# Segment 0 split in halves, and the constants of dt and S5 and the first S5 tables queued later

## The chip, the core and the metric

The kernel runs on one core of one Trainium2 chip. The metric is the device time of one execution in microseconds; the median of several runs counts. The core's engines work from queues of their own, each in order: TensorE (PE, with its weight loads PEld), VectorE (DVE), ScalarE (ACT), GpSimd (POOL) and SyncE (SP), which here issues the transfers.

## What is computed

One layer of a hybrid recurrent decoder: RMSNorm of x, one input projection, three branches (an SSD scan, an RG-LRU scan, an S5 complex scan), each gated, then the output projection with the residual and a final RMSNorm. There are 2048 prompt rows and 64 sample rows of width 1024.

```python
h = rmsnorm(x, p['norm_g'])
proj = h @ p['w_in']
z, xbc, dt_raw, lru_x, lru_gate, s5_u, s5_gate = jnp.split(proj, SPLITS, axis=-1)
...
dt = jax.nn.softplus(dt_raw + p['ssd_dt_bias'])
a = -jnp.exp(p['ssd_a_log'])
...
ys5, s5_hr, s5_hi = s5_mixer(s5_u, p['s5_lambda_re'], p['s5_lambda_im'], p['s5_log_dt'], ...)
...
out = jnp.concatenate([y_ssd, y_lru, y_s5], axis=-1) @ p['w_out']
return x + out, ...
```

`s5_mixer` takes constants from its parameters alone (exp, sin and cos of `lambda * delta`, their powers, `bbar`); nothing of x goes into them. The same holds for `a` and for the scaled weights of dt.

## The kernel before

**Segments and blocks.** The rows are cut into `SEGS`: segments 0 to 3 of 512 prompt rows and segment 4 of the 64 sample rows, taken in the order `ORD = [0, 4, 1, 2, 3]`. The input projection's weights come as blocks of 128 columns (`Block`, line 181). A block is loaded as f32 into one of two `w32` buffers, its largest value (lines 194, 197) goes through TensorE (`bcast_scales`, the matmul of line 168) to a scale, and ScalarE (line 205) and VectorE (line 206) write its high and low f16 parts into `whl`, of which six exist. `w_ahead` traces the next block. `in_proj` (line 235) multiplies one block with one segment: per slice k of 128 input channels three matmuls (lines 247 to 249), high with high, high with low, low with high, 24 in all, into one of three PSUM banks.

**A segment's input.** `x_load` (line 263) loads tiles of 128 rows. `x_split` (line 289) takes them in pairs: ScalarE squares and sums (line 305), `rsqrt_of` makes the scale, VectorE applies it (line 308). Then for each k all four tiles are transposed on TensorE into one PSUM bank (line 312), ScalarE writes `XH` (line 314) and VectorE the rest `XL` (line 315), which frees the bank.

**The order of tracing.** In the loop over `ORD` (line 1247) segment i + 1 is split ahead of the S5 inputs of segment i (`s5_u`, line 791) and of some gates (`zgates`, whose VectorE step is line 363). At s == 2, that is i = 3, the kernel traces `x_split(3)`, the last split, and then `dt_w` (line 419: decay constants and scaled weights of dt) and `s5_consts` (line 809: exponentials by `exp_acc`, two Sin calls at lines 845 and 846, powers by `cmul` with lines 154 to 159, and `renorm`). At s == 3 it traces `s5_tables(sa, 0)` (line 901), the tables of the first S5 core, ahead of segment 3's S5 inputs: products on GpSimd (lines 912 to 935), transposes and small matmuls on TensorE (lines 944 and 950), eight transfers `TR<-K` (line 962), and the table `W` on VectorE and ScalarE (lines 967 to 980, with lines 978 and 979 for its upper halves). After the loop come `dt_seg` (small matmuls), `dt_finish` (the softplus, up to line 463), gates, `dt_sums` (from line 476), gates, and the four S5 cores (`s5_core`, line 997, first matmul line 1008). Tables b + 1 are traced behind core b; their scratch tiles share two slots, so their first product (line 912) needs a scratch tile of the tables before to be released.

**What sets the order on an engine.** The source's order is a priority, not the order itself: a planner (`schedule_with_timeline_sim=True`) goes through a simulated run, gives each engine the first-traced instruction among those that are ready at that moment, and writes each engine's queue from that. So work that depends on little is issued long before its place in the source. `behind(*ins)` (line 272) adds an edge from each instruction traced in it to the given one on the same engine: it is issued after that one. Instructions on other engines get no edge.

Of the kernel before, what the change touches and what calls it, by code (L numbers as in the profile page):

```python
# [8 lines left out]
F32 = mybir.dt.float32  # L9
# [12 lines left out]
D = 1024  # L22
KD = 8
# [19 lines left out]
def hymba_step_kernel(  # L43
# [191 lines left out]
    def in_proj(w, s):  # L235
# [10 lines left out]
        for k in range(KD):  # L246
            P.matmul(ps[:, :n], lhsT=w[:, 0, k, :], rhs=XH[s][:, k, :], start=(k == 0), stop=False)  # L247
            P.matmul(ps[:, :n], lhsT=w[:, 0, k, :], rhs=XL[s][:, k, :], start=False, stop=False)  # L248
            P.matmul(ps[:, :n], lhsT=w[:, 1, k, :], rhs=XH[s][:, k, :], start=False, stop=(k == KD - 1))  # L249
# [39 lines left out]
    def x_split(s):  # L289
# [8 lines left out]
        for q in range(0, len(rows), 2):  # L298
            pair = rows[q:q + 2]
            m = len(pair)  # L300
            ss = tmp.tile([128, 2], F32, name="ss2", tag="ss2", bufs=4)
            rs = tmp.tile([128, 2], F32, name="rs2", tag="rs2", bufs=4)
            for i, xt in enumerate(pair):
                sq = st.tile([128, D], BF16, name="xsq", tag="yhl", bufs=3)
                A.activation(out=sq[:n], in_=xt[:n], func=AF.Square, scale=D ** -0.5, accum_out=ss[:n, i:i + 1])
            rsqrt_of(rs[:n, :m], ss[:n, :m], n, XSC, m)()
            for i, xt in enumerate(pair):
                V.tensor_scalar(xt[:n], xt[:n], rs[:n, i:i + 1], None, op0=ALU.mult)
        for k in range(KD):
            ps = bank(*((ptp, "tp") if k % 2 else (pss, "gy"[k // 2 % 2])), "ps_xt")  # L310
            for i, xt in enumerate(rows):
                P.transpose(ps[:, 128 * i:128 * i + n], xt[:n, k * 128:(k + 1) * 128], id32[:n, :n])
            g = gcol[:, k:k + 1]
            A.activation(out=XH[s][:, k, :sn], in_=ps[:, :sn], func=AF.Copy, scale=g)
            V.scalar_tensor_tensor(XL[s][:, k, :sn], ps[:, :sn], g, XH[s][:, k, :sn], op0=ALU.mult, op1=ALU.subtract)
# [931 lines left out]
    for i, s in enumerate(ORD):  # L1247
        if 0 < i < 4:
            if i > 1:
                x_load(ORD[i + 1], xp)  # L1250
            x_split(ORD[i + 1])
        if s == 2:
            dt_w(dp)
            s5_consts(sk)
        if s == 3:
            xa.close()
            sa = pool(s5, "s5a", "left")
            tabs = s5_tables(sa, 0)
# [6 lines left out]
        zgates(GA[i])  # L1265
    for s in ORD:
        dt_seg(s)
# [196 lines left out]
```

## Time and profile before

| | us |
|---|---|
| median of 3 runs | 1663.81 |
| the runs | 1662.63 to 1663.87 |
| profiled execution | 1667.2 |
| its span | 1665.5 |
| busy: PE, DVE, ACT, POOL | 1580.5, 1114.9, 858.8, 542.2 |

The profile is of one execution; times count from its start. Rows of an engine in order of time give start, duration, source line, output <- inputs, count, and in brackets how long the engine sat idle before and what released it. Rows for windows give the busy time of PE, PEld, DVE, ACT and POOL, the granted TensorE clock as a share of full speed (PEclk), the mean busy share of the DMA engines and GB/s. A matmul's duration has its pipeline in it; neighbouring ones overlap.

### The profile page before, as it was taken

Reading aid. Unit: us, or ns where it says so; the run is one execution under the profiler, and the core shown is the slowest. Engines: PE = TensorE matmul, PEld = TensorE weight load, DVE = VectorE, ACT = ScalarE, POOL = GpSimd, SP = SyncE. Lnnn points to the kernel's source line nnn. Section 1 sums busy time; section 2 is a strip of 40 time slices with the busy share of each in tenths; the row PEclk is TensorE's granted clock in tenths of the full one; section 3 lists DMA queues with packets and bytes.
Section 4 is the critical chain, followed back from the end, with each engine's and each line's share of the span. In section 5 each row is a group of like instructions: output and inputs, shape, how many; then the busy total and the mean of one; then the engine's idle time right before and its main releaser. Section 6 shows DMA issues by size and latency. Waiting matters only on the chain.

```text
span 1665.5 us, 26647 instructions
## 1 busy us (share of the span) xinstructions
PE 1580.5 (95%) x9474; PEld 814.7 (49%) x9474; DVE 1114.9 (67%) x2643; ACT 858.8 (52%) x1913; POOL 542.2 (33%) x822
## 2 busy tenths in 40 slices
PE   6899899988989998999999999999999999999998
PEld 3554444444434444455555555555554544444443
DVE  7843579899486676578978967676777774533332
ACT  7834424434597776656656745466756352322210
POOL 1213316784032021155647545444444400000000
PEclk9999899999989999999999999999999999999999
DMA  7512322322232534333435433243335452533100
GB/s 242 136 47 52 97 101 90 90 84 88 85 118 73 150 112 112 99 86 98 141 111 140 134 96 101 65 134 109 108 114 160 136 184 92 187 102 101 45 26 33
DMA packets 143942, 178.18 MB, mean 107 GB/s; under 512 B 66424, under 2 KB 92480, under 8 KB 143808
## 3 DMA queue, kind: packets, MB, share of 16 engines
q1 hardware_dynamic: 143808, 176.47, 35.4%
q8 instruction: 75, 1.23, 0.3%
q14 instruction: 59, 0.48, 0.1%
HBM read 126.57 MB, written 48.69 MB: 105 GB/s over the span
## 4 chain that ended last, share of the span: by engine, by line
PE 44%; DVE 8%; ACT 3%; issue 2%; DMA 2%; POOL 1%; SPq 0%; POOLq 0%; ACTq 0%; DVEq 0%
PE ps_o L1180 7%; PE ps_o L1178 7%; PE ps_o L1179 7%; PE ps_mm L248 6%; PE ps_mm L247 6%; PE ps_mm L249 6%; DVE x L355 3%; PE ps_y L568 1%; PE ps_s L573 1%; PE ps_y L571 1%; PE ps_s L618 1%; DVE e L531 1%; PE ps_tp L545 1%; DVE x L642 1%; PE ps_o L1212 1%
## 5 line engine op out<-in xcount | busy, mean ns | idle before, releaser
L247 PE MATMUL ps_mm<-xh,whl 128*128 128x512 f16 x1280 | 493.7, 386 | 13.7 <-DVE pz L363 8.9
L249 PE MATMUL ps_mm<-xh,whl 128*128 128x512 f16 x1280 | 492.5, 385 | 0.9 <-DVE whl L206 0.9
L248 PE MATMUL ps_mm<-xl,whl 128*128 128x512 f16 x1280 | 493.1, 385 | 0.0
L248 PEld LDWEIGHTS <-whl 128*128 128x128 f16 x1600 | 155.9, 99 | 164.7 <-issue 33.6
L249 PEld LDWEIGHTS <-whl 128*128 128x128 f16 x1600 | 156.3, 99 | 152.1 <-issue 16.5
L247 PEld LDWEIGHTS <-whl 128*128 128x128 f16 x1600 | 159.2, 101 | 145.8 <-issue 16.3
L355 DVE SCALAR_TENSOR_TENSOR x<-raw,hcols,x 128x512 f32<-128x512 f32 x192 | 173.7, 905 | 37.1 <-ACT x L353 35.0
L1179 PE MATMUL ps_o<-wo,yt 128*128 128x512 f16 x512 | 194.0, 379 | 0.0
L1178 PE MATMUL ps_o<-wo,yt 128*128 128x512 f16 x512 | 193.9, 379 | 0.0
L1180 PE MATMUL ps_o<-wo,yt 128*128 128x512 f16 x512 | 193.7, 379 | 0.0
L1193 ACT ACTIVATE yt<-y,rsc 128x256 f16<-128x256 f32 (+1 forms) x144 | 56.8, 477 | 103.1 <-PE ps_o L1180 83.1
L524 ACT ACTIVATE e<-bcq,acum 128x128 f32<-128x128 f32 (+1 forms) x272 | 85.7, 386 | 34.5 <-PE ps_y L568 31.6
L538 POOL TENSOR_TENSOR ce<-ce,x 128x512 f32<-128x512 f32 x60 | 82.5, 1381 | 44.5 <-DMA ce<-eT 35.6
L641 ACT ACTIVATE th<-x 128x512 f32<-128x512 f32 x64 | 40.2, 628 | 101.5 <-DVE x L355 101.3
L1202 DVE SCALAR_TENSOR_TENSOR res<-ps_o,rsu,res 128x512 f32<-128x512 f32 x32 | 24.0, 750 | 98.6 <-PE ps_o L1180 98.6
L1367 ACT ACTIVATE yo<-res 128x1024 f32<-128x1024 f32 x16 | 16.8, 1050 | 133.0 <-DVE res L1202 133.0
L363 DVE SCALAR_TENSOR_TENSOR pz<-th,ps_mm 128x512 f32<-128x512 f32 x64 | 43.6, 682 | 54.3 <-ACT th L362 53.8
L1179 PEld LDWEIGHTS <-yt 128*128 128x128 f16 x512 | 50.2, 98 | 60.1
L1178 PEld LDWEIGHTS <-yt 128*128 128x128 f16 x512 | 50.2, 98 | 60.1
L1180 PEld LDWEIGHTS <-yt 128*128 128x128 f16 x512 | 50.1, 98 | 60.2 <-issue 0.2
L362 ACT ACTIVATE th<-ps_mm,sc_out 128x512 f32<-128x512 f32 x64 | 43.7, 683 | 63.5 <-PE ps_mm L249 63.0
L531 DVE TENSOR_TENSOR e<-e,gm 128x512 f32<-128x512 f32 (+1 forms) x68 | 55.9, 821 | 27.7 <-POOL gm L530 22.0
(449 smaller groups left out, 3018.6 us busy)
## 6 DMA issues: line engine op xcount, KB each, us to landing
w<-in_w_blk_dram SPq DMA_DIRECT2D x40, 512.0 KB
bcq<-aT SPq DMA_DIRECT2D x64, 256.0 KB
y<-ysp SPq DMA_DIRECT2D x16, 1024.0 KB
ce<-eT SPq DMA_DIRECT2D x60, 256.0 KB
xt<-in_x_dram SPq DMA_DIRECT2D x16, 512.0 KB
ysp<-x SPq DMA_DIRECT2D x32, 256.0 KB
wo<-in_w_out_dram SPq DMA_DIRECT2D x16, 512.0 KB
res<-in_x_dram SPq DMA_DIRECT2D x16, 512.0 KB
```

The lines of the kernel that those rows point to most:

```text
L247: P.matmul(ps[:, :n], lhsT=w[:, 0, k, :], rhs=XH[s][:, k, :], start=(k == 0), stop=False)
L248: P.matmul(ps[:, :n], lhsT=w[:, 0, k, :], rhs=XL[s][:, k, :], start=False, stop=False)
L249: P.matmul(ps[:, :n], lhsT=w[:, 1, k, :], rhs=XH[s][:, k, :], start=False, stop=(k == KD - 1))
L355: V.scalar_tensor_tensor(o, tap[j], w[j], o, op0=ALU.mult, op1=ALU.add)
L362: A.activation(out=th, in_=ps, func=AF.Tanh, scale=un2)
L524: A.activation(out=e[:n, h, :n], in_=bcq[:n, h, :n], func=AF.Relu, scale=-1.0, bias=acum[:n, c, 4 * g + h:4 * g + h + 1])
L531: V.tensor_tensor(e[:n, :, :n], e[:n, :, :n], gm.unsqueeze(1).to_broadcast([n, 4, n]), op=ALU.mult)
L538: G.tensor_tensor(ce[:, :, :n], ce[:, :, :n], CT[:, q0:q0 + n].unsqueeze(1).to_broadcast([128, 4, n]), op=ALU.mult)
L1178: P.matmul(ps, lhsT=h, rhs=w[:, 0, c], start=(k == 0), stop=False)
L1179: P.matmul(ps, lhsT=h, rhs=w[:, 1, c], start=False, stop=False)
L1180: P.matmul(ps, lhsT=l, rhs=w[:, 0, c], start=False, stop=(k == nk - 1))
L1193: A.activation(out=hl[:, k, 0, :n], in_=r[:, k, :n], func=AF.Copy, scale=c)
```

## The change

Three edits. `x_split` takes segment 0 in two halves of two row tiles, each with its own transposes, `XH` and `XL`, and `in_proj` multiplies the first block with segment 0 in the same two halves of 256 columns; all other segments and blocks stay as they were. `x_split` returns its last ScalarE and VectorE instruction, and `dt_w` and `s5_consts` are traced `behind` those of segment 3. `s5_tables(sa, 0)` is traced after the loop instead of at the start of its last pass.

```diff
@@ -243,10 +243,12 @@
                     b.finish()
             b.left = b.left or (b.w is w and s == 3)
         ps = bank(pmm, "mm", "ps_mm")
-        for k in range(KD):
-            P.matmul(ps[:, :n], lhsT=w[:, 0, k, :], rhs=XH[s][:, k, :], start=(k == 0), stop=False)
-            P.matmul(ps[:, :n], lhsT=w[:, 0, k, :], rhs=XL[s][:, k, :], start=False, stop=False)
-            P.matmul(ps[:, :n], lhsT=w[:, 1, k, :], rhs=XH[s][:, k, :], start=False, stop=(k == KD - 1))
+        first = s == 0 and w is WB[W_ORDER[0]].w
+        for c in (slice(0, n // 2), slice(n // 2, n)) if first else (slice(0, n),):
+            for k in range(KD):
+                P.matmul(ps[:, c], lhsT=w[:, 0, k, :], rhs=XH[s][:, k, c], start=(k == 0), stop=False)
+                P.matmul(ps[:, c], lhsT=w[:, 0, k, :], rhs=XL[s][:, k, c], start=False, stop=False)
+                P.matmul(ps[:, c], lhsT=w[:, 1, k, :], rhs=XH[s][:, k, c], start=False, stop=(k == KD - 1))
         return ps[:, :n]
 
     def seg_tile(tag, name, s, pool, w=SG, bufs=None, wsmp=NS):
@@ -295,24 +297,29 @@
             XL[s] = xpool.tile([128, KD, SG], F16, name="xl", tag="xs")
         n = min(128, sn)
         rows = [XT[s0 + o] for o in range(0, sn, 128)]
-        for q in range(0, len(rows), 2):
-            pair = rows[q:q + 2]
-            m = len(pair)
-            ss = tmp.tile([128, 2], F32, name="ss2", tag="ss2", bufs=4)
-            rs = tmp.tile([128, 2], F32, name="rs2", tag="rs2", bufs=4)
-            for i, xt in enumerate(pair):
-                sq = st.tile([128, D], BF16, name="xsq", tag="yhl", bufs=3)
-                A.activation(out=sq[:n], in_=xt[:n], func=AF.Square, scale=D ** -0.5, accum_out=ss[:n, i:i + 1])
-            rsqrt_of(rs[:n, :m], ss[:n, :m], n, XSC, m)()
-            for i, xt in enumerate(pair):
-                V.tensor_scalar(xt[:n], xt[:n], rs[:n, i:i + 1], None, op0=ALU.mult)
-        for k in range(KD):
-            ps = bank(*((ptp, "tp") if k % 2 else (pss, "gy"[k // 2 % 2])), "ps_xt")
-            for i, xt in enumerate(rows):
-                P.transpose(ps[:, 128 * i:128 * i + n], xt[:n, k * 128:(k + 1) * 128], id32[:n, :n])
-            g = gcol[:, k:k + 1]
-            A.activation(out=XH[s][:, k, :sn], in_=ps[:, :sn], func=AF.Copy, scale=g)
-            V.scalar_tensor_tensor(XL[s][:, k, :sn], ps[:, :sn], g, XH[s][:, k, :sn], op0=ALU.mult, op1=ALU.subtract)
+        step = 2 if s == 0 else 4
+        for q0 in range(0, len(rows), step):
+            part = rows[q0:q0 + step]
+            for q in range(0, len(part), 2):
+                pair = part[q:q + 2]
+                m = len(pair)
+                ss = tmp.tile([128, 2], F32, name="ss2", tag="ss2", bufs=4)
+                rs = tmp.tile([128, 2], F32, name="rs2", tag="rs2", bufs=4)
+                for i, xt in enumerate(pair):
+                    sq = st.tile([128, D], BF16, name="xsq", tag="yhl", bufs=3)
+                    A.activation(out=sq[:n], in_=xt[:n], func=AF.Square, scale=D ** -0.5, accum_out=ss[:n, i:i + 1])
+                rsqrt_of(rs[:n, :m], ss[:n, :m], n, XSC, m)()
+                for i, xt in enumerate(pair):
+                    V.tensor_scalar(xt[:n], xt[:n], rs[:n, i:i + 1], None, op0=ALU.mult)
+            c = slice(128 * q0, 128 * q0 + n * len(part))
+            for k in range(KD):
+                ps = bank(*((ptp, "tp") if k % 2 else (pss, "gy"[k // 2 % 2])), "ps_xt")[:, 0:n * len(part)]
+                for i, xt in enumerate(part):
+                    P.transpose(ps[:, 128 * i:128 * i + n], xt[:n, k * 128:(k + 1) * 128], id32[:n, :n])
+                g = gcol[:, k:k + 1]
+                last = [A.activation(out=XH[s][:, k, c], in_=ps, func=AF.Copy, scale=g),
+                        V.scalar_tensor_tensor(XL[s][:, k, c], ps, g, XH[s][:, k, c], op0=ALU.mult, op1=ALU.subtract)]
+        return last
 
 
     tails = const.tile([128, 20, 27], F32, name="tails")
@@ -1248,14 +1255,14 @@
         if 0 < i < 4:
             if i > 1:
                 x_load(ORD[i + 1], xp)
-            x_split(ORD[i + 1])
+            xs_last = x_split(ORD[i + 1])
         if s == 2:
-            dt_w(dp)
-            s5_consts(sk)
+            with behind(*xs_last):
+                dt_w(dp)
+                s5_consts(sk)
         if s == 3:
             xa.close()
             sa = pool(s5, "s5a", "left")
-            tabs = s5_tables(sa, 0)
             S.dma_start(out=st_all, in_=conv_st)
             lru_const(dp)
         for b in range(4):
@@ -1263,6 +1270,7 @@
             if s == 3:
                 w_ahead()
         zgates(GA[i])
+    tabs = s5_tables(sa, 0)
     for s in ORD:
         dt_seg(s)
     dta = dt_finish(dp)
```

## Rows read from the trace of the kernel before

**Rows 1.** windows of 50 us: us, busy time (instructions) of each engine, PEclk, DMA share

```profile
100.00:150.00 50.00, 50.00 (x292) 25.78 (x289) 11.22 (x29) 14.48 (x21) 12.73 (x17) 1.00 0.18 50
150.00:200.00 50.00, 42.61 (x455) 23.95 (x454) 25.81 (x76) 27.55 (x65) 18.39 (x22) 0.88 0.35 86
350.00:400.00 50.00, 50.00 (x281) 25.96 (x279) 47.04 (x122) 22.84 (x73) 31.34 (x52) 1.00 0.32 96
```

**Rows 2.** TensorE in order of time: start us, us, line, what [idle before <-releaser]

```profile
10.39 1.09 PE L312 MATMUL ps_xt<-id,xt 128*128 128x128 f32 x4 [0.70 <-DVE sc_m L115]
18.63 0.58 PE L247 MATMUL ps_mm<-xh,whl 128*128 128x512 f16 x1 [0.31 <-ACT xh L314]
20.98 0.63 PE L248 MATMUL ps_mm<-xl,whl 128*128 128x512 f16 x1
24.29 0.38 PE L248 MATMUL ps_mm<-xl,whl 128*128 128x512 f16 x1
```

**Rows 3.** groups by line, 0 to 60 us: form, count, busy us, mean ns

```profile
L315 DVE SCALAR_TENSOR_TENSOR xl<-ps_xt,gcol,xh 128x512 f16<-128x512 f32 x16 | 11.5, 744 | 0.4 <-ACT xh L314 0.4
L315 DVE SCALAR_TENSOR_TENSOR xsm<-ps_xt,gcol,xsm 128x64 f16<-128x64 f32 x8 | 2.2, 278 | 2.3 <-ACT xsm L314 2.3
L206 DVE SCALAR_TENSOR_TENSOR whl<-w,sc_out,whl 128x1024 f16<-128x1024 f32 x5 | 6.4, 1277 | 0.8 <-ACT whl L205 0.8
```

**Rows 4.** TensorE in order of time, 50 to 80 us

```profile
54.95 0.19 PE L247 MATMUL ps_mm<-xsm,whl 128*128 128x64 f16 x1 [1.23 <-ACT u L796]
75.44 3.20 PE L312 MATMUL ps_xt<-id,xt 128*128 128x128 f32 x12 [3.22 <-DVE xl L315]
```

**Rows 5.** VectorE in order of time, 71 to 76 us

```profile
71.54 2.05 DVE L308 TENSOR_SCALAR xt<-xt,rs 128x1024 f32<-128x1024 f32 x2
73.51 1.13 DVE L158 TENSOR_TENSOR uw<-s_tt 128x16 f32<-128x16 f32 x1
74.65 1.40 DVE L315 SCALAR_TENSOR_TENSOR xl<-ps_xt,gcol,xh 128x512 f16<-128x512 f32 x2
```

**Rows 6.** windows around two stalls, columns as in rows 1

```profile
72.00:84.00 12.00, 8.66 (x33) 4.60 (x32) 11.97 (x33) 7.59 (x13) 5.78 (x5) 0.72 0.11 44
174.00:184.00 10.00, 9.57 (x35) 4.36 (x36) 4.87 (x12) 4.57 (x8) 5.58 (x4) 0.66 0.47 131
```

**Rows 7.** ScalarE in order of time, 162 to 175 us

```profile
162.39 1.14 ACT L205 ACTIVATE whl<-w,sc_out 128x1024 f16<-128x1024 f32 x1
173.23 1.06 ACT L197 ACTIVATE whl<-w 128x1024 bf16<-128x1024 f32 x1 [0.77 <-DMA w<-in_w_blk_dram]
```

**Rows 8.** TensorE in order of time, 168 to 175 us

```profile
174.43 0.59 PE L168 MATMUL ps_sc<-w_mx,ones 128*128 128x1 f32 x2 [5.64 <-DVE whl L206]
```

**Rows 9.** VectorE in order of time, 119 to 171 us

```profile
119.37 2.73 DVE L315 SCALAR_TENSOR_TENSOR xl<-ps_xt,gcol,xh 128x512 f16<-128x512 f32 x4 [3.39 <-ACT xh L314]
147.62 0.16 DVE L154 TENSOR_TENSOR tW<-W,wpw 128x4 f32<-128x4 f32 x1
161.65 5.18 DVE L979 SCALAR_TENSOR_TENSOR W<-W,wpw,tW 128x128 f32<-128x128 f32 x4 [1.82 <-ACT tW L978]
166.75 2.25 DVE L206 SCALAR_TENSOR_TENSOR whl<-w,sc_out,whl 128x1024 f16<-128x1024 f32 x1
170.16 0.86 DVE L979 SCALAR_TENSOR_TENSOR W<-W,wpw,tW 128x128 f32<-128x128 f32 x3
```

**Rows 10.** GpSimd in order of time, 161 to 182 us

```profile
161.17 1.17 POOL L912 TENSOR_TENSOR tC<-Ct,Ap 128x576 f32<-128x576 f32 x1 [7.79 <-DMA TR<-K]
180.56 1.26 POOL L935 TENSOR_TENSOR AB<-tD 128x512 f32<-128x512 f32 x1
```

**Rows 11.** VectorE and TensorE in order of time, 221 to 236 us

```profile
221.22 0.44 DVE L463 TENSOR_TENSOR dtz<-dt_all,hd 128x272 f32<-128x272 f32 x1
226.23 0.59 PE L476 MATMUL ps_dt<-dtz,tri 128*128 128x256 f32 x2
235.89 1.12 PE L1008 MATMUL ps_s<-u,sl 128*64 128x264 f32 x8
```

## The prediction

> **What bounds the kernel now.** I read the windows of equal length first, then TensorE in order of time around each gap they show, then the engine that each gap names. From 350 us TensorE is busy in 50.00 of 50 us [rows 1], and so it is in most later windows: there it sets the pace. The change works ahead of that, where time is lost. Between 150 and 200 us it is busy in 42.61 with a mean granted clock of 0.88, against 50.00 and 1.00 between 100 and 150 us [rows 1]. Three places hold the loss. **The start:** the first projection matmul begins at 18.63 us, although transposes of the first two row tiles begin at 10.39 [rows 2]; `x_split` waits for all four tiles before any slice of `XH` exists. **The gap at 72 us:** 3.22 us of waiting for `XL` on VectorE [rows 4]; behind it the mean clock of 12 us is 0.72 [rows 6]. Below full speed it is at the lower of its two levels (1.2 of 2.4 GHz, so 0.5), and 12 x (1 - 0.72) = 3.4 us of work are lost on top. **The gap at 169 us:** 5.64 us [rows 8], then a clock of 0.66 over 10 us [rows 6], another 3.4 us.
>
> **The profiled execution** took 1667.2 us around a span of 1665.5; the median of the runs is 1663.8, 3.4 less. I make the sum against 1667.2 and take the same difference off the median.
>
> **A, the first segment in halves.** The transposes of tiles 0 and 1 stay where they are. They end at about 11.5 [rows 2]; with a half-width copy on ScalarE behind what it has queued there (`whl` of the same block among it) I put the first matmul at about 13 us. 512 columns at 2.4 GHz are 0.21 us, so a group of 24 matmuls is 5.1 us; its first half, 2.6 us of work, now fits before 18.63. The matmuls from 20.98 stand with 0.63 us in their rows and those from 24.29 with 0.38 [rows 2]: seven of them ran at the lower level, and earlier work may lift the clock before they come, up to 7 x 0.21 = 1.5 us. Between 18.63 and 20.98 there is at most 1.2 us of waiting that may go as well. So the upper end is 5.3. Against it stands VectorE, nearly full at that time: L315 takes 744 ns for 512 columns and 278 for 64 [rows 3], which makes 0.48 us for 256; sixteen of them cost 7.7 us in place of 5.9. If VectorE ends the second half, that is -1.7. About as many microseconds of constants leave the same queue, so I take **+3.5**, the 2.6 and part of the clock.
>
> **B, the constants queued behind the last split.** `behind` holds only instructions of ScalarE and VectorE: some 211 small VectorE ones of `dt_w` and `s5_consts` with a few of ScalarE. The six loads on SP's queue, GpSimd's memsets, copies and products and one TensorE matmul aren't held; the loads stay as early as now and cost nothing new, and the rest waits for its data. At 72 us VectorE had the row scaling L308 and then L158, a 16-column product of the constants that took 1.13 us, before `XL` L315 could start at 74.65 [rows 5]; without L158 and L159 it starts 1.1 us earlier. That is the lower end; the whole gap with its clock is 3.2 + 3.4 = 6.6. GpSimd's products of the constants leave this place too, and I take **+5**. ScalarE loses the two Sin calls, with the table loads that they bring, from a stretch in which TensorE once waits 1.23 us for it [rows 4]: 0 to 1.2, taken **+1**. Where the constants go, behind the last `XL` of segment 3 (the four that begin at 119.37 [rows 9], earlier by what is gained), VectorE is busy 11.22 of 50 us [rows 1]; 211 instructions of about the 0.16 us of a 4-column product [rows 9] are 34 us of busy time, where 39 of 50 are free. Queued behind them are the gates' `pz` (L363), for which TensorE's banks wait; three banks of 5.1 us each cover them, and I take 0 with 1 us as the other end.
>
> **C, the first tables behind the seg-3 projections.** The gap at 169 us is a chain. ScalarE ends `whl` L205 at 163.5 [rows 7]; VectorE's L206 for the same block starts only at 166.75, because four L979 of the tables take 5.18 us in front of it (three later ones take 0.86, so 0.29 each), and itself takes 2.25 [rows 9]. It frees the buffer for the next load, which ScalarE waits for until 173.23 [rows 7], and TensorE's L168 comes at 174.43. L206 takes 1.28 us earlier on [rows 3]; started at 163.5 it would end 4.2 us earlier and leave 1.4 of the gap. So 4.2 without the clock, 9.0 with everything, 0 if other table work lands there. I take **+6**, the 4.2 and half of the clock.
>
> **E, what the tables will hit instead.** GpSimd's work for the second tables starts at 161.17, when the transfers `TR<-K` of the first have released their scratch tile, and its twelve large instructions last until 180.56 and beyond [rows 10]. Later first tables make it later. In the old place it ran against L979 and L206; each of the four L979 lost (5.18 - 4 x 0.29) / 4 = 1.0 us there [rows 9]. In the new place it meets the softplus of dt, which ends at 221.22 with TensorE's sums waiting until 226.23 [rows 11]; the last product of that chain is over at 221.9, so 4.3 us of room. Half of the twelve hitting it costs 6 - 4.3 = 1.7 us and, if the clock falls, 3.4 more: **-5**, between 0 and 12 - 4.3 + 3.4 = 11.1.
>
> **Sum:** 3.5 + 5 + 1 + 6 - 5 = 10.5 us, 1656.7 for the profiled execution, 1653.3 for the median.
>
> **The rivals.** *No collision:* the planner lets TensorE take the tables' transposes early (it fills gaps between groups, as now), GpSimd is done before the softplus, and E is 0: 10.5 + 5 = 15.5 off, 1648. For it: nothing after 121 us but order keeps the tables back.
> *Full collision:* all twelve hit the softplus, E is 11.1, 1659. For it: dt's matmuls follow the first tables directly in the source. The Trainium skill says in "SBUF — State Buffer", section "Who interferes with whom", that a two-input VectorE instruction and a GpSimd one share a port pair which one of them holds to its end while the other fully blocks; by that rule each of the twelve stops one instruction, and this rival is the result. The L979 rows agree, 1.0 us lost by each.
> *Slower:* the W tables' VectorE chain, which now runs from 147.62 to 171.02 [rows 9], 23.4 us, is queued behind the softplus. That would end near 221.7 - 9.5 + 6 = 218 and W at 241.6, where the first S5 core's matmuls come at 235.89 now [rows 11]: 5.7 us later than before and 3.4 for the clock, 1673. It decides from the point where the last L979 ends later than about 230. Against it: VectorE has free time behind 119 us, and the constants' 34 us of busy time end by about 160 even if nothing in them overlaps.
> *A gap of C's size elsewhere:* TensorE's queue is ordered anew from 12 us on, and 9.0 us come back at another block: 1662.
> *The halves do nothing:* VectorE is the pace, A is 0: 1657.
>
> **Chances.** Forecast 0.46, no collision 0.16, full collision 0.16, slower 0.09, gap elsewhere 0.07, halves idle 0.06. 0.2% of the time, 3.3 us, is about what a measurement of this kernel can tell from no change. Faster than 1660.5 are the forecast, the first, the last and most of the full collision: 0.72. The gap elsewhere and the rest of those give within 0.2%: 0.15. Slower: 0.13, with a little for gaps that add up. The range goes from all gains at their upper ends (5.3 + 1.2 + 6.6 + 9.0 = 22 off, 1642) to the gap elsewhere plus a loss in A, 1666; it leaves out the slower rival.
>
> **What would show it.** In the new profile the first projection matmul stands at 12 to 14 us with 256 columns; no gap of 3 us stands near 72; no Sin table load before the last split; L206 of the blocks loaded behind segment 3 takes 1.3 us and L168 waits under 2 us for it; L912 of the second tables comes at 170 or later, and the softplus rows grow from 0.44 to over 1 us beside it. The first S5 core starts near 225. I am wrong if the first matmul still waits until 18 us, if the gap at 169 us only moves, or if the core starts no earlier than 235.

## The result and the profile after

The changed kernel takes 1672.05 us, median of 5 runs, where the kernel before takes 1663.81: a ratio of 1.0058, 95% interval 1.0046 to 1.0071. Measured once more (the run *changed*) it was 1.0044 (1.0027 to 1.0061). It is slower by about half a per cent, clear of the noise; forecast were 1653.3, between 1642 and 1666. The profiled execution took 1672.05 us around a span of 1670.3 (before: 1667.2 around 1665.5). That of before lay 3.4 us above its median and that of after on it, so the two traces differ by 4.9 us, not by the 8.2 of the medians.

To see where the time went I add up, in windows of 10 us, what TensorE loses: its idle time and its busy time x (1 - PEclk), the work that a lower clock costs. From kernel to kernel these sums follow the spans within 4 us. One part is missing in them: PEclk stands at 1.00 in the first windows, though matmuls still have the long rows of the lower level there (0.63 us at 20.98 in before [rows 2], 0.42 at 15.39 in after, below). Half of TensorE's busy time up to the clock's first record (23.7 us in before, 19.1 in after) is an estimate of what the first column leaves out: 4.8 us and 3.9.

```
lost on TensorE, us   0-100  100-150  150-200  200-240  240-450  450-1640   sum
before                 23.5      0.0     11.8      0.6     24.2      42.2  102.3
after                  17.5      0.5     16.2     10.9     20.2      42.2  107.5
difference             -6.0     +0.5     +4.4    +10.3     -4.0       0.0   +5.2
forecast               -9.5      0.0     -6.0     +5.0      0.0       0.0  -10.5
```

The third and the fourth stretch hold two things each. From 150 to 180 us, where the gap at 169 was, before loses 7.3 and after 9.3. Behind that come dt's small matmuls (L452, after L459; 189 to 199 us before, 183 to 192 after): with the lower clock behind them they cost 5.1 in before (180 to 210 us) and 7.0 in after (180 to 200). So the gap at 169 was replaced by one that is 2.0 us larger, and the 10.9 from 200 on are new.

The windows of after, columns as in [rows 1], show the same: where [rows 1] had a whole 50 us from 100 on, 0.46 are missing, 150 to 200 got worse, and of the 40 us from 200 on TensorE works 31.31.

```profile
100.00:150.00 50.00, 49.54 (x246) 24.27 (x244) 38.09 (x177) 17.27 (x25) 16.02 (x26) 1.00 0.14 38
150.00:200.00 50.00, 40.65 (x425) 22.66 (x426) 36.30 (x139) 22.84 (x58) 12.79 (x16) 0.83 0.35 86
200.00:240.00 40.00, 31.31 (x186) 15.86 (x184) 30.69 (x68) 9.51 (x17) 8.25 (x7) 0.87 0.25 83
```

The windows around stalls: the one at 72 us is nearly gone against [rows 6] (11.28 busy of 12, clock 1.00), and a new one stands at 190 to 210.

```profile
72.00:84.00 12.00, 11.28 (x60) 5.86 (x59) 9.65 (x17) 10.37 (x16) 1.91 (x4) 1.00 0.15 44
...
190.00:210.00 20.00, 9.52 (x101) 5.50 (x101) 19.48 (x38) 5.27 (x20) 10.68 (x11) 0.67 0.11 29
```

TensorE of after in order of time (L249 is before's L247, L318 its L312). The first projection matmul, 256 columns, stands at 12.89 instead of 18.63 [rows 2], and from 19.16 on such a matmul takes 0.27 us instead of 0.42, the full speed that before has in its row at 24.29 [rows 2]; the wait of 3.22 us at 72 [rows 4] is 0.71. The wait of 5.64 us at 169 [rows 8] isn't there, but one of 5.17 stands at 157 to 162 and one of 8.69 at 201 to 210. Both are put down to L115, the first VectorE step of a weight block's scale: it reads a sum that TensorE has left in a bank, and TensorE's next use of that bank waits for it.

```profile
12.89 0.37 PE L249 MATMUL ps_mm<-xh,whl 128*128 128x256 f16 x1 [0.28 <-ACT xh L320]
...
15.39 0.42 PE L250 MATMUL ps_mm<-xl,whl 128*128 128x256 f16 x1
...
19.16 0.27 PE L250 MATMUL ps_mm<-xl,whl 128*128 128x256 f16 x1
...
76.69 1.31 PE L318 MATMUL ps_xt<-id,xt 128*128 128x128 f32 x8 [0.71 <-DVE xl L321]
...
162.39 0.56 PE L168 MATMUL ps_sc<-w_mx,ones 128*128 128x1 f32 x2 [5.17 <-DVE sc_m L115]
...
209.96 0.58 PE L249 MATMUL ps_mm<-xh,whl 128*128 128x512 f16 x1 [8.69 <-DVE sc_m L115]
```

**The first new gap.** ScalarE had one block's squares at 146.5 and the next one's at 151.7, and then waited 11.01 us for the scale of the first, which L115 begins at 162.09; the matmul L168 at 162.39 is that of the next block and waited for the same L115 to free the bank:

```profile
146.35 0.18 ACT L197 ACTIVATION_READ_ACCUMULATOR whl<-w 128x1 f32 x1
...
151.51 0.19 ACT L197 ACTIVATION_READ_ACCUMULATOR whl<-w 128x1 f32 x1
162.71 1.15 ACT L205 ACTIVATE whl<-w,sc_out 128x1024 f16<-128x1024 f32 x1 [11.01 <-DVE sc_out L107]
```

VectorE in the same time, and again from 191 us. Up to 162.6 it has the constants' chain of dependent 16- and 32-column steps (L154 to L159, L809 to L812), with L115 in the middle of its last round. Some of the steps take 0.16 us, others 0.9 to 1.3 in the rows shown. From 191 on the same shows in W's chain (L986, before's L979), where eight take 4.23 us, and in the softplus: L467, L468, L123 and L124 take 1.94, 1.53, 1.04 and 1.14 us, where they take 0.44, 0.49, 0.30 and 0.30 in the run *held* below. L470 behind them has its usual 0.44 ([rows 11] has the same for L463).

```profile
155.51 1.24 DVE L155 TENSOR_TENSOR s_tt<-uw 128x16 f32<-128x16 f32 x1
156.68 0.16 DVE L156 TENSOR_TENSOR s_tt<-uw 128x16 f32<-128x16 f32 x1
...
158.97 1.29 DVE L810 TENSOR_TENSOR rn_t<-rn_t 128x16 f32<-128x16 f32 x1
...
162.09 0.15 DVE L115 TENSOR_SCALAR sc_m<-ps_sc 128x1 int32<-128x1 int32 x1
...
191.03 4.23 DVE L986 SCALAR_TENSOR_TENSOR W<-W,wpw,tW 128x128 f32<-128x128 f32 x8 [0.17 <-ACT tW L985]
195.18 1.94 DVE L467 TENSOR_TENSOR dtz<-d 128x272 f32<-128x272 f32 x1
...
197.15 1.53 DVE L468 SCALAR_TENSOR_TENSOR dtz<-dtz,dtun,hd 128x272 f32<-128x272 f32 x1
...
200.07 1.04 DVE L123 TENSOR_SCALAR ex_r<-sp_az 128x272 f32<-128x272 f32 x1
...
201.16 1.14 DVE L124 TENSOR_SCALAR ex_k<-ex_r 128x272 f32<-128x272 f32 x1
...
209.75 0.16 DVE L115 TENSOR_SCALAR sc_m<-ps_sc 128x1 int32<-128x1 int32 x1
...
211.34 0.67 DVE L370 SCALAR_TENSOR_TENSOR pz<-th,ps_mm 128x512 f32<-128x512 f32 x1
...
226.90 0.44 DVE L470 TENSOR_TENSOR dtz<-dt_all,hd 128x272 f32<-128x272 f32 x1
```

GpSimd, beside them: the first tables' products lie from 135.04 to 160.2 with a pause from 145.7 to 155.4, the second tables' (161.17 to 181.8 in [rows 10]) from 192.65 to 215.0. The long rows of VectorE stand beside these and not in the pauses.

```profile
135.04 1.15 POOL L919 TENSOR_TENSOR tC<-Ct,Ap 128x576 f32<-128x576 f32 x1
...
155.45 1.27 POOL L939 TENSOR_TENSOR AB<-tD 128x512 f32<-128x512 f32 x1 [9.73 <-DVE CA L931]
...
158.97 1.26 POOL L942 TENSOR_TENSOR AB<-tD 128x512 f32<-128x512 f32 x1
...
192.65 1.29 POOL L919 TENSOR_TENSOR tC<-Ct,Ap 128x576 f32<-128x576 f32 x1 [8.86 <-DMA dm<-in_s_d_dram]
...
213.62 1.34 POOL L942 TENSOR_TENSOR AB<-tD 128x512 f32<-128x512 f32 x1
```

I count as stretched the VectorE instructions of up to 272 columns that take over 0.6 us, and add what each takes above 0.18. Before, the constants (40 to 100 us) have 2 of them, 1.6 us in all. After, between 120 and 164 us, it is 14 and 11.8 us.

### The profile page after: what moved, and what is told of

Read it like the earlier page. It is cut to its first block, busy times and chain, and to the rows that moved or that the text cites. A ratio compares the mean times of both kernels' runs of the same rounds, so it can differ in the third digit from the quotient of the medians.

```text
span 1670.3 us, 26716 instructions
## 1 busy us (share of the span) xinstructions
PE 1579.0 (95%) x9498; PEld 814.9 (49%) x9498; DVE 1132.6 (68%) x2651; ACT 863.3 (52%) x1925; POOL 539.6 (32%) x822
## 3 DMA queue, kind: packets, MB, share of 16 engines
q8 instruction: 75, 1.23, 0.3%
## 4 chain that ended last, share of the span: by engine, by line
PE 47%; DVE 8%; ACT 4%; DMA 3%; issue 2%; POOL 1%; SPq 0%; ACTq 0%; POOLq 0%; DVEq 0%
PE ps_o L1185 7%; PE ps_o L1186 7%; PE ps_o L1187 7%; PE ps_mm L249 6%; PE ps_mm L250 6%; PE ps_mm L251 6%; DVE x L362 3%; PE ps_y L575 2%; PE ps_s L580 1%; PE ps_y L578 1%; PE ps_s L625 1%; DMA y<-ysp 1%; PE ps_tp L552 1%; DMA ce<-eT 1%; DVE e L538 1%
## 5 line engine op out<-in xcount | busy, mean ns | idle before, releaser
L249 PE MATMUL ps_mm<-xh,whl 128*128 128x512 f16 (+1 forms) x1288 | 494.2, 384 | 28.3 <-DVE sc_m L115 15.9
L251 PE MATMUL ps_mm<-xh,whl 128*128 128x512 f16 (+1 forms) x1288 | 493.9, 383 | 0.2 <-DVE whl L206 0.2
L250 PE MATMUL ps_mm<-xl,whl 128*128 128x512 f16 (+1 forms) x1288 | 493.7, 383 | 0.0
L249 PEld LDWEIGHTS <-whl 128*128 128x128 f16 x1608 | 160.1, 101 | 148.1 <-issue 17.7
L205 ACT ACTIVATE whl<-w,sc_out 128x1024 f16<-128x1024 f32 x40 | 45.7, 1142 | 45.8 <-DVE sc_out L107 45.8
```

Of the source, the lines that this page charges most:

```text
L205: A.activation(out=w[:, 0], in_=self.r, func=AF.Copy, scale=su[:, 0:1])
L249: P.matmul(ps[:, c], lhsT=w[:, 0, k, :], rhs=XH[s][:, k, c], start=(k == 0), stop=False)
L250: P.matmul(ps[:, c], lhsT=w[:, 0, k, :], rhs=XL[s][:, k, c], start=False, stop=False)
L251: P.matmul(ps[:, c], lhsT=w[:, 1, k, :], rhs=XH[s][:, k, c], start=False, stop=(k == KD - 1))
```

## The experiments

The theory after the reading (theory one): the constants' late chain, traced ahead of the blocks' scales, stands in front of L115 (first gap), and it carries the second gap too, since it makes the tables late. The rival: the tables' later place does. Theory two, which the later texts speak of, was formed after the run chain: the place in the source decides nothing at the first gap; the chain is late because GpSimd's products stretch its steps. Theory three, on the halves, stands in the text of quiet_whole. One table for all runs: ratio to the kernel before with its interval, the loss on TensorE by stretch as above (one execution each), the start of segment 3's transposes and of the first S5 core, in us.

```
                ratio (95%)              0-100 100-150 150-200 200-240 240-450 450-1640   sum  seg.3  core
before          1                         23.5    0.0    11.8     0.6    24.2     42.2   102.3  111.7 235.9
halves          1.0010 (0.9995-1.0024)    23.9    0.0    13.5     0.6    23.6     43.4   105.1  110.4 234.7
consts          1.0021 (1.0008-1.0034)    16.0    0.6    21.5     1.1    24.2     39.3   102.7  103.4 237.8
tables          1.0012 (0.9996-1.0027)    23.1    0.0    10.5    10.3    19.4     40.5   103.8  111.2 241.0
halves_consts   1.0018 (1.0005-1.0030)    17.9    0.0    22.2     3.8    21.7     37.1   102.6  105.6 242.4
halves_tables   1.0025 (1.0009-1.0041)    23.9    0.0    10.4     8.3    21.7     44.0   108.4  110.1 238.6
consts_tables   1.0034 (1.0021-1.0046)    17.0    0.6    16.0     8.3    20.2     47.6   109.8  103.7 238.8
changed         1.0044 (1.0027-1.0061)    19.4    0.0    15.0    11.6    19.1     42.3   107.4  107.4 244.0
held            1.0043 (1.0022-1.0064)    18.7    0.0    16.8     0.0    27.8     41.7   105.0  105.4 233.0
chain           1.0052 (1.0037-1.0067)    17.9    0.0    16.2    11.1    19.8     44.2   109.1  105.2 241.6
quiet           0.9986 (0.9975-0.9998)    20.1    0.0    13.9     4.5    18.5     46.6   103.7  106.5 239.0
quiet_again     1.0001 (0.9987-1.0015)    18.0    0.0    16.0     3.2    19.7     43.3   100.1  104.4 238.0
quiet_whole     1.0004 (0.9991-1.0017)    17.3    0.0    17.1     3.4    22.2     43.0   103.0  103.5 232.3
quiet_held      1.0007 (0.9994-1.0020)    20.3    0.0     8.3     0.0    29.8     47.4   105.8  107.4 225.2
mid             0.9995 (0.9986-1.0004)    18.5    4.3    12.8     1.0    23.5     41.0   101.1  105.6 235.2
wl              0.9980 (0.9967-0.9992)    22.4    0.0     7.7     0.0    22.1     41.2    93.5  110.5 233.9
mid_wl          0.9992 (0.9978-1.0005)    18.6    3.9     5.9     0.0    21.6     45.3    95.4  106.3 232.5
halves_wl       0.9989 (0.9973-1.0004)    23.6    0.0     7.9     0.0    21.2     46.4    99.1  110.5 233.8
```

Executions of one kernel lie up to 7 us from their median, once 12 (the profiled one of quiet was its slowest, 1668.1 at a median of 1662.9), so a single sum of this table is good to a few us; single stretches differ by more than that where it matters. The stretch behind 450 us moves by as much from run to run as the parts do ahead of it. Ratios measured twice, of the changed kernel (1.0058, 1.0044) and of quiet (0.9986, 1.0001), came out 0.0014 and 0.0015 apart, so a difference of that size between two rows tells little.

**The parts alone and in pairs.** Out of the changed kernel one or two of these were undone: the halves,

```diff
-        first = s == 0 and w is WB[W_ORDER[0]].w
+        first = False
...
-        step = 2 if s == 0 else 4
+        step = 4
```

the constants, and the tables:

```diff
-            with behind(*xs_last):
-                dt_w(dp)
-                s5_consts(sk)
+            dt_w(dp)
+            s5_consts(sk)
...
             sa = pool(s5, "s5a", "left")
+            tabs = s5_tables(sa, 0)
...
-    tabs = s5_tables(sa, 0)
```

> The kernel before with the first segment in halves and nothing else. Theory one (the halves do what was forecast, and the loss sits in the two later places): first matmul at about 13 us, everything up to 150 us some 3 to 4 us earlier, 1659 to 1661. Rival (the halves let the planner order the later work anew, and that costs what it brings): first matmul at 13 us as well, but 1664 or more, with new waits behind 240 us.

> The kernel before with the constants behind the last split and nothing else; the first tables keep their old place in the source. Theory one (the constants' late end carries the loss: their chain stands on VectorE ahead of the blocks' scale steps, and the tables, which need them, come late by themselves): no gap at 72 us, a gap of 5 us or more between 150 and 170 us, the second tables' GpSimd work at 190 us or later and the softplus stretched by it, 1669 to 1675. Rival (the later tables of the source carry the loss): the gap at 72 us goes, the first S5 core starts before 233 us, 1657 to 1661.

> The kernel before with the first tables traced behind the projections and nothing else; the constants are ready by 100 us as before. Theory one (the constants carry the loss): the gap at 169 us shrinks from 5.6 to under 2 us, the second tables' GpSimd work starts before 185 us, 1658 to 1663. Rival (the tables' place in the source carries it): second tables' GpSimd work at 190 us or later, softplus rows over 1 us, first S5 core at 240 us or later, 1667 to 1672.

> The changed kernel with the first tables back in their old place: halves and constants, without the third part. Theory one (halves alone lose their gain in the gap at 72 us, which grew, and the constants' new place closes that gap): better than the sum of the two alone, 6 us gained by 100 us as in the whole change, a gap of 5 us or more left between 150 and 170, dt's sums at 224 to 227, 1664 to 1667. Rival (the parts simply add up, 1.0010 and 1.0021): 1.003, 1668 to 1670, and the third part adds only 0.002 to 0.003 to it.

> The changed kernel with the constants back in their old place: halves and tables, without the second part. Theory two: the constants end by 100 us beside little GpSimd work, the gap of 5.2 us before 162 is not there; the gap at 72 and the 7 to 9 us wait at 205 stay; first S5 core at 239 to 242, 1665 to 1669. Rival (parts add up, 1.0010 and 1.0012): 1.0022, 1667 to 1668. Rival (the second part brings most of the loss to the whole): 1.001 or less.

> The changed kernel with the first segment whole again: constants and tables, without the halves. Theory two (the halves' gain reaches the end only where VectorE isn't the pace at 72 us, so it counts here): 2 to 3 us slower than the whole change, 1673 to 1676. Rival (parts add up): 1.0033 to the kernel before, 1669 to 1671, faster than the whole change, since the halves only cost.

> The changed kernel once more, on the chip of the two others, so that they have it beside them. Every theory: 1.0035 to 1.0065. Below 1.003, the parts' sum (1.0043) and the whole couldn't be told apart from a smaller loss.

No part alone is faster. The totals of halves and tables are nearest to the rivals (1666.6 and 1666.5 us), though the new waits behind 240 us that the rival of halves named aren't there (23.6 us lost, before 24.2). consts lies between the two (1667.8), and halves_consts, at 1668.3, has the rival's total with a ratio below the rival's 1.003 and dt's sums at 231.5, later than forecast. What each part does by stretch is plainer. *consts* gains 7.5 us up to 100, where 6 were forecast for it, and loses 9.7 more between 150 and 200. There the first tables' transposes wait, since GpSimd's product waits for a VectorE step queued behind the chain (from 150 to 180 us it loses 10.2, before 7.3), and from 180 to 200 dt's small matmuls lose 11.3 (before 4.5), waiting 6.4 us for ScalarE's `d` (L462), `pz` and L115. TensorE's waits of consts, 140 to 170 us (engine, line, waited for: us in total, times, longest):

```profile
PE ps_tp L951 <- POOL AB L939: 4.5, 1, 4.5
```

*tables* has none of that: from 150 to 180 us it loses nothing, so the gap at 169 is gone as forecast. But dt's small matmuls lose 10.5 from 180 to 200, its second tables' products start at 190.10, it loses 9.7 more between 200 and 240 and gains 4.8 back by 450. Its waits at 150 to 240 us and a row of its W chain (eight L986, 0.29 us each when alone as in [rows 9]):

```profile
PE ps_mm L249 <- DVE sc_m L115: 7.3, 1, 7.3
```

```profile
190.41 6.39 DVE L986 SCALAR_TENSOR_TENSOR W<-W,wpw,tW 128x128 f32<-128x128 f32 x8 [0.25 <-ACT tW L985]
```

So the first gap belongs to the constants' place and the second to the tables' place. Why dt's small matmuls lose more with either part was not tried. The halves bring nothing: the kernels with and without them differ by -0.0003 to +0.0024, in the six pairs of the table. The ratios nearly add up: 0.0010 + 0.0021 + 0.0012 is 0.0043, measured 0.0044 and 0.0058; the rival of adding parts held for halves_tables and consts_tables (1.0022 and 1.0033 expected, 1.0025 and 1.0034 measured), and my expectation for consts_tables, slower than the whole, failed (1670.0 us, expected 1673 to 1676).

**Is it the order in the source?** The ten rounds of the chain that only W's table needs were traced behind the projections:

```diff
-        for _ in range(3):
+        def powers():
+            for _ in range(3):
...
+    K5["powers"]()
     tabs = s5_tables(sa, 0)
```

> The changed kernel with one part of the constants, the ten dependent steps of the powers that only W's table needs (about 110 small VectorE instructions), traced behind the projections in place of among the other constants. Theory one (the gap of 5.2 us before 162 is L115 of a block's scale standing behind this chain on VectorE): TensorE's wait at 150 to 170 us under 2 us, the loss between 150 and 200 us under 9 us in place of 16.3 (idle 9.4 and clock 6.9). The chain itself then comes from 160 us on and W's table behind it, into the softplus, so up to 10 us may be lost again between 200 and 240; 1662 to 1674, and only the first loss tells. Rival (GpSimd's products or the late tables themselves hold VectorE and TensorE up at that place): the wait at 150 to 170 stays above 4 us.

The rival was right as far as it goes. VectorE of chain in order of time: the chain lies where it was, with L115 in its last round again, and the wait is 5.0 us. The planner puts a step that is ready onto an idle engine, wherever it stands in the source. So the edit moved nothing, and my theory that its being traced first holds L115 up has fallen; that L115 stands behind the chain in VectorE's queue is untouched by it.

```profile
159.84 1.12 DVE L811 TENSOR_SCALAR rn_t<-rn_t 128x16 f32<-128x16 f32 x1
...
162.58 0.15 DVE L115 TENSOR_SCALAR sc_m<-ps_sc 128x1 int32<-128x1 int32 x1
```

**Is it GpSimd beside the chain?** A GpSimd copy that reads the last power, and the first tables behind it:

```diff
+        powered = sc.tile([128, 16], F32, name="powered")
+        K5["powered"] = G.tensor_copy(powered, wpw[:, 0, :, 7])
...
-    tabs = s5_tables(sa, 0)
+    with behind(K5["powered"]):
+        tabs = s5_tables(sa, 0)
```

> The changed kernel with one more GpSimd copy of 16 columns that reads the last of the constants' powers, and the first tables traced behind it: GpSimd's products of the first tables can't run beside the constants' chain on VectorE. Theory two (the place in the source decides nothing, as moving the chain showed; the chain of small steps ends some 12 us late because GpSimd's products stretch 15 of them from 0.17 to about 1 us, and L115 has its slot behind it): the time above 0.18 us of the small steps between 120 and 164 us falls from 12.4 to under 5 us, the chain ends at 152 to 156 instead of 162.6, and TensorE's wait for L115 falls from 5.2 to under 1 us. The tables then come 5 to 15 us later and fall on the softplus with more, so the total may still be 1668 to 1676. Rival (L115 waits for the order alone): the chain ends earlier, the wait before 170 stays over 4 us.

> The run quiet once more, on the chip of quiet_whole, to have the two side by side: 0.9975 to 0.9998 of the kernel before by every theory.

> The changed kernel with the first tables held behind the constants' last power, as in the run quiet, and the first segment whole again. Theory three (the halves bring 1.5 us of projection work by 20 us and lose it again by 50 us, because VectorE, not TensorE, is the pace there and the halves give it more instructions): segment 3's transposes at 103.4 to 105 us in place of 106.5, the total the same as quiet or up to 3 us below it, 1659 to 1663. Rival (the halves' gain is real and is what makes quiet faster than the kernel before): 2 to 4 us above quiet, 1665 to 1667.

Theory two, formed after chain, holds. The stretched steps between 120 and 164 us are 2 with 0.9 us in place of 14 with 11.8, the chain ends at 152.1 in place of 162.6, and TensorE has no wait at all between 140 and 172 us. VectorE of quiet, last step of the chain and the L115 behind it, and then GpSimd:

```profile
151.88 0.20 DVE L900 COPY wpw<-uw 128x32 f32<-128x32 f32 x1
151.98 0.15 DVE L115 TENSOR_SCALAR sc_m<-ps_sc 128x1 int32<-128x1 int32 x1
```

```profile
152.14 0.21 POOL L902 COPY powered<-wpw 128x16 f32<-128x16 f32 x1 [15.15 <-DVE sc_m L115]
152.31 1.17 POOL L921 TENSOR_TENSOR tC<-Ct,Ap 128x576 f32<-128x576 f32 x1
```

The totals, 0.9986 and 1.0001, were better than the 1668 to 1676 us that I thought possible for quiet: one copy takes back 0.0043 to 0.0072 of the changed kernel's ratios, although the second wait is still there (6.6 us in quiet, ending at 202, so that the border at 200 us cuts it in two; 7.4 in quiet_again). The repeat missed its own range, though, 0.9975 to 0.9998: the hold brings the changed kernel back to the kernel before, and whether it is faster than that stays open. quiet_whole, the same without the halves, is 1.0004 beside 1.0001 on the same chip, 0.8 us more, which fits neither text's total; the halves bring nothing that can be told here either. Its transposes of segment 3 come at 103.5, as theory three has it, before the 104.4 of quiet_again.

**Is it GpSimd beside the softplus?** A GpSimd copy of the softplus' result, and the later tables behind it; then both holds together:

```diff
         V.tensor_tensor(z, dt_all, nega.unsqueeze(1).to_broadcast([128, 17, 16]), op=ALU.mult)
+        seen = tmp.tile([128, 16], F32, name="seen", tag="seen", bufs=1)
+        DT["seen"] = G.tensor_copy(seen, z[:, 16, :])
...
-            tabs = s5_tables(sa, b + 1)
+            with behind(DT["seen"]):
+                tabs = s5_tables(sa, b + 1)
```

> The changed kernel with one more GpSimd copy of 16 columns that reads the result of the softplus, and the second tables (and the third and fourth) traced behind it, so that their GpSimd products can't run beside the softplus. Theory one (the meeting of GpSimd's products with W's chain and the softplus makes the 5 us lost between 190 and 231 us and the 8.7 us wait at 205): softplus rows back to 0.3 to 0.5 us, the wait at 205 us under 4 us, dt's sums at 224 to 227 in place of 231.2, 1664 to 1667 in place of 1672. Rival (VectorE's queue is simply long there: W's chain and the block's scale steps stand in one order whatever GpSimd does): sums at 230 or later, 1670 or more; a further loss is possible where the second tables come too late for the second S5 core.

> The changed kernel with both holds: the first tables' GpSimd work behind the constants' last power, and the second tables' behind the result of the softplus. Theory two (the whole loss is VectorE's small steps beside GpSimd's products, in two places, and each hold takes one of them away): neither of the waits for L115 above 2 us, the softplus over by 211 to 215, dt's sums at 215 to 219, idle and clock between 150 and 240 us under 14 us in place of 27 in the changed kernel; 1657 to 1661. Rival (the second hold gives back in the S5 core what it gains, as in the changed kernel with that hold alone, where the loss between 240 and 450 us was 27.9 in place of 20.3): sums as early, 1662 or more.

The mechanism holds, the forecast of the total doesn't (1672.0 us, where 1664 to 1667 were expected). In held the softplus steps are back at 0.44 and 0.30 us and it ends at 218.5 in place of 227.3; the loss between 200 and 240 is 0.0 in place of 10.9, the first S5 core comes 8.2 us earlier. VectorE of held:

```profile
195.81 0.44 DVE L139 SCALAR_TENSOR_TENSOR sp_az<-dtz 128x272 f32<-128x272 f32 x1
196.29 0.30 DVE L123 TENSOR_SCALAR ex_r<-sp_az 128x272 f32<-128x272 f32 x1
...
218.05 0.44 DVE L470 TENSOR_TENSOR dtz<-dt_all,hd 128x272 f32<-128x272 f32 x1
```

But the products now run until 239.8, beside the first S5 core, whose own products (L1028, L1029) take their turn among them, and 240 to 450 us loses 27.8 in place of 20.2. GpSimd of held:

```profile
218.99 1.16 POOL L921 TENSOR_TENSOR tC<-Ct,Ap 128x576 f32<-128x576 f32 x1
...
237.43 0.73 POOL L1029 TENSOR_TENSOR v<-v,x 128x256 f32<-128x256 f32 x1
238.12 1.65 POOL L944 TENSOR_TENSOR AB<-tD 128x512 f32<-128x512 f32 x1
```

quiet_held shows the same more sharply: dt's sums at 215.5, the first core at 225.2 (10.7 earlier than before the change), and 29.8 lost behind 240. The rival of quiet_held, that the second hold is given back in the S5 core, was right, and held shows the same.

**The places of before, mended otherwise.** *mid* waits for the second segment's split instead of the third's (with the halves, tables in the old place). *wl* is the kernel before with the second tables held behind the copy of W's last column; *mid_wl* and *halves_wl* combine them.

```diff
             xs_last = x_split(ORD[i + 1])
+            if i == 2:
+                xs_mid = xs_last
...
-            with behind(*xs_last):
+            with behind(*xs_mid):
```

```diff
-        G.tensor_copy(K5["wl"][:, :, pr], W[:, :, :, 255])
+        K5["done"] = G.tensor_copy(K5["wl"][:, :, pr], W[:, :, :, 255])
...
-            tabs = s5_tables(sa, b + 1)
+            with behind(*(K5["done"],) * (b == 0)):
+                tabs = s5_tables(sa, b + 1)
```

> The kernel before with the first segment in halves and the constants behind the split of the second segment (XL ends near 80 us) in place of the third's; the first tables in their old place. Theory one (the gain up to 100 us is real, and it was lost only by the constants' late end): constants over by 130 us, no gap at 72, the loss between 150 and 200 us as before the change (7.4 and 4.4), first S5 core at 230 to 232, 1657 to 1661. Rival (each part gives back later what it gains, wherever the constants stand): 1664 or more.

> The kernel before, with one edit that the change doesn't have: the second tables are held on GpSimd behind the copy of W's last column, the last step of the first tables, so that GpSimd's products can't run beside W's chain. Theory one (the forecast's reading of the gap at 169 us, L979 stretched from 0.29 to 1.3 us by GpSimd in front of L206): all L979 at 0.3 us, the gap under 2 us, GpSimd's products at about 171 to 191 us and so before the softplus, 1655 to 1660. Rival (the gap is VectorE's order alone): L979 short, the gap still 4 us or more, 1663 or more.

> The kernel before with three edits: the first segment in halves, the constants behind the second segment's split, and the second tables held on GpSimd behind the first tables' last column of W; the first tables in their old place. Theory two (constants and W's chain both away from GpSimd's large products, softplus free): the gaps at 72 and 169 both under 2.5 us, first S5 core at 229 to 232, ratio 0.996 to 0.998, 1658 to 1661. Rival (what is gained ahead of 240 us is lost in the S5 core, where 1 us less has shown as nothing): ratio 0.999 or more.

> The kernel before with the halves, and the second tables held behind the first tables' last column of W. Without the halves this hold gave 0.998. Theory two (the halves' early start is used up in the gap at 72 us as long as the constants stand there): the gap at 72 us grows as in the halves alone, the total is the same as without the halves, 0.997 to 0.9995. Rival (the halves' gain reaches the end once the gap at 169 us is gone): 0.996 or less.

*wl* is the only run beside quiet whose interval lies below 1 (0.9980), and it shows that the forecast read the gap at 169 us rightly: the four L979 take 1.23 us in place of the 5.18 of [rows 9], L206 waits for nothing but ScalarE's part, GpSimd begins when W is done, and TensorE waits 1.81 us in place of 5.64 [rows 8]. Its lead of 0.0020 is little more than repeats differ by, and it was measured once. VectorE, GpSimd and TensorE of wl:

```profile
160.41 1.23 DVE L979 SCALAR_TENSOR_TENSOR W<-W,wpw,tW 128x128 f32<-128x128 f32 x4 [1.83 <-ACT tW L978]
162.33 1.28 DVE L206 SCALAR_TENSOR_TENSOR whl<-w,sc_out,whl 128x1024 f16<-128x1024 f32 x1 [0.69 <-ACT whl L205]
```

```profile
164.79 0.19 POOL L981 COPY wl<-W 128x8 f32<-128x8 f32 x1 [31.98 <-DVE sc_m L116]
165.23 1.16 POOL L912 TENSOR_TENSOR tC<-Ct,Ap 128x576 f32<-128x576 f32 x1 [0.24 <-issue]
```

```profile
169.37 0.38 PE L168 MATMUL ps_sc<-w_mx,ones 128*128 128x1 f32 x2 [1.81 <-ACT whl L197]
```

Expected were 1655 to 1660 us, measured 1661.6 beside 1664.9. *mid* has the early gain and the old gap at 169, and a new loss of 4.3 us at 100 to 150, where the constants (10 stretched steps, 9.4 us) meet the third split: 0.9995, nearer to the rival. *mid_wl* should have added up the two and is 0.9992, as its rival had it. *halves_wl* came out as expected. Up to 450 us mid_wl, wl and halves_wl lose 50.0, 52.2 and 52.8, where before loses 60.1; why only 1.2 to 3.3 us of that reach the total stays open.

## Why the prediction was wrong, step by step

**A, the halves, +3.5: failed.** The first matmul and the full speed from 19 us came as forecast. Counted from the matmuls begun, at full speed, the halves alone had 1.7 us of projection work behind them at 20 us where before had 0.2, but 20.9 against 20.7 at 50 us. By segment 3's transposes (the column seg.3) they are 1.3 us ahead of before, and where the constants have moved they are behind: 105.6 against 103.4 (consts), 104.5 in after against 103.7 (consts_tables). The step that failed is taking TensorE's early work as a gain while VectorE sets the pace: the term was +3.5, and 1.3 or less came of it. Its lower end, -1.7, allowed for that. Sixteen half-width `XL` steps took 469 ns each in place of eight at 744 [rows 3], groups by line of after, 0 to 60 us:

```profile
L321 DVE SCALAR_TENSOR_TENSOR xl<-ps_xt,gcol,xh 128x256 f16<-128x256 f32 x16 | 7.0, 469 | 0.0
```

That VectorE's pace is what takes the gain back is read from this and from the wait for `XL` at 72 us, which grew in halves; it was not tried by itself. TensorE's waits of halves, 60 to 90 us (before: one of 3.22, [rows 4]):

```profile
PE ps_xt L318 <- DVE xl L321: 6.7, 2, 5.7
```

**B, the gap at 72, +5 and +1: right.** consts gained 7.5 us up to 100, and the wait in after is 0.71 us.

**The constants' new place, 0 to -1: the step that failed most.** I counted 34 us of busy time into 39 us of room and looked at `pz` alone as what stands behind. Two things were missed. The steps run beside GpSimd's products, 11.8 us of stretch where E charged such a meeting only to the softplus; and L115, which frees the bank that TensorE's next sum or projection needs, has its place behind them. A new gap stands where the old one was: 9.3 us from 150 to 180 where before lost 7.3 and the forecast took 6 off. The run quiet shows the cause: with GpSimd's products behind the chain that loss is 3.0.

**C, the gap at 169, +6: right about the gap, wrong about the net.** L206 takes 1.28 us behind segment 3 and the old wait is gone, in tables without any loss left from 150 to 180. But the later tables are what brings the second gap (tables alone: +9.7 at 200 to 240). The sum also has no term for dt's small matmuls, a fourth place of loss beside the three that the prediction names: 5.1 us before, 7.0 after, 10.5 in tables.

**E, -5: the mechanism was right, the size was too small.** The loss between 200 and 240 us grew by 10.3, near the upper end of 11.1. I let half of the twelve products hit, and didn't count W's chain, which meets them too (eight L986 at 4.23 us), nor that L115 stands among the softplus steps, which is the 8.69 us wait. The Trainium skill, "SBUF — State Buffer", section "Who interferes with whom", has the two-input VectorE instruction fully blocked while GpSimd holds the shared port pair; the trace agrees (0.17 to 1.24 us, and 0.17 again in quiet), and also with its statement that an instruction with one SBUF input, outside the 2-port modes, isn't affected: `pz`, with its other input in PSUM, takes 0.67 us at 211.34 beside GpSimd's products.

**The rivals.** Full collision (1659), gap elsewhere (1662) and idle halves (1657) all came true, and together: 1653.3 + 6 + 9 + 3.5 is 1671.8. That this meets the measured median is partly luck: it leaves out the 4.0 us that came back behind 240 and the 2.0 more of dt's matmuls. The first two have one cause, GpSimd's products beside small VectorE steps, and I gave them chances as if one excluded the other; the range followed from that. Two sums in it are off as well: 1666 is the gap elsewhere with A at nothing, and with A's loss of 1.7 it would be 1667.5; and 0.72 leaves only 0.04 of the full collision's 0.16 for the faster side, not most of it. Neither would have reached 1672. The slower rival had another mechanism, W queued behind the softplus, which did not happen (W was done at 195.3), so that its 241.6 for the first core meets the measured 241.2 by luck. Behind 240 us the later start gave 4.0 us back, which no step had; and in held and quiet_held an earlier start lost more. That the tables' products meet the S5 core there is shown by their rows; how much of the give-back it makes stays open.

## What to carry to other kernels

Before a chain of small VectorE steps is moved, look at what GpSimd does in the new place and at who stands behind the chain in VectorE's queue; one hold on GpSimd's side (0.0043 to 0.0072) was worth more than any of the three edits. A step that only reads a TensorE sum can hold a bank, so it belongs to the list of who waits. Rivals with one cause come together: price the joint case, and let the range reach to it.

## What the runs showed of the hardware

A 16- or 32-column VectorE step of 0.17 to 0.20 us takes 0.6 to 1.4 us beside GpSimd products of 0.64 to 1.4 us: 14 of them cost 11.8 us. A step of 272 columns went from 0.44 to 1.94 us, less in proportion to its own length. Steps with a single f32 tensor in SBUF were stretched like those with two, which I had not counted: the 272-column L123 takes 0.30 us in held and 1.04 after the change (200.07 us), and the 16-column L811 takes 1.12 in chain.
